# The biases of the second attention, made by GpSimd instead of ScalarE

## The chip, the cores and the metric

The kernel runs on one core of one Trainium2 chip. The metric is the time of one execution on the device, in microseconds. The core has TensorE (PE in the profile), VectorE (DVE), ScalarE (ACT), GpSimd (POOL) and SyncE (SP), which here issues most of the DMAs. Each engine works through its own instructions in order and waits for others by semaphores.

## The reference

The program is one block of a transformer on 256 tokens of width 1024, in float32: a norm, one wide projection, three attentions of 8 heads of 64 (a: stick-breaking, b: "forgetting", c: with a linear position bias), a gate on each, an output projection, and an MLP. Only the second attention matters here:

```
c = lax.cumsum(jax.nn.log_sigmoid(f_logit.astype(jnp.float32)), axis=2)
logits = einsum('bhqd,bhkd->bhqk', qb, kf) * scale + (cq[..., :, None] - c[..., None, :])
p = jax.nn.softmax(jnp.where(causal, logits, NEG_INF), axis=-1)
```

To each logit of query q and key k a bias c[q] - c[k] is added, and keys behind the query are masked.

## The kernel before

Every float32 matrix is split into a high part, rounded to the type float32r, and a low part that holds the rest; three products (high-high, high-low, low-high) are summed in PSUM. So every operand costs two instructions ahead of its matmul: a rounding copy on ScalarE (line 107 for weights, 299 for queries and keys, 361 for attention weights, 379 for attention outputs) and a subtraction on VectorE (lines 110, 300, 362, 380).

Weights come in pieces of 1 MB over SP's queue (line 96, `raw`, two buffers). `pump` splits them ahead of use into up to 7 halves.

The beginning (lines 151 to 331) is in an order written out by hand. Behind it the program text is a list of steps: projections of the pieces of a, b and c one after another, and at given steps the stages of the attention pairs (two heads at a time, four pairs per branch). `forget_bias(pair)` is called at the steps 10, 12, 15 and 17, two steps before the first stage of its pair. The final order on each engine is decided by the framework's planner, from priorities that follow the program text and its own estimates of the costs. It also decides when a buffer is taken.

`forget_terms` makes c: the negated cumulative sums go to DRAM as 8 rows (`c_rows`), and the sums, transposed, to `cq`, a column per head and half of the queries. `forget_bias(pair)` loads for each of two heads its row, broadcast to 128 partitions (`pb`, name `rows`, two buffers, SP's queue, line 491). For each half t of the queries it makes the bias of (t+1) x 128 keys: ScalarE adds the column `cq` to the row (line 497), then GpSimd masks the diagonal block (line 499, `affine_select`). The bias tiles have four buffers, one per head, so the third pair's tiles take those of an earlier pair, once VectorE has read them; four small tiles of the beginning and the third attention's biases (`alibi_bias`, made by GpSimd at line 506) use the same buffers.

`softmax_pair` reads the biases: at line 432 VectorE adds the bias to the logits in PSUM and takes the row minimum of the negated sum, and at line 434 ScalarE takes the exponential.

GpSimd's other work in this part is the zeroing of the padded query and key tiles (lines 288 and 289). Later it has only four short things.

Of the kernel before, what the change touches and what calls it, by code (L numbers as in the profile page):

```python
# [10 lines left out]
AF = mybir.ActivationFunctionType  # L11
ALU = mybir.AluOpType
PSUM = bass.MemoryType.PSUM

P = 128
# [22 lines left out]
def hybrid_attention_block(ctx, tc, x, norm_mix, w_in, b_forget, w_branch, w_out,  # L38
# [4 lines left out]
    nc = tc.nc  # L43
# [406 lines left out]
    forget, bias = {}, {"b": {}, "c": {}}  # L450
# [35 lines left out]
    def forget_bias(pair):  # L486

        rows, cq = forget["c"]
        pb = act.tile([P, 2, S], F32, name="rows", tag="rows", bufs=2)
        for s in range(2):  # L490
            nc.sync.dma_start(pb[:, s], rows[2 * pair + s].partition_broadcast(P))
        for s in range(2):
            h = 2 * pair + s
            b = act.tile([P, 384], F32, name="bias", tag="bias", bufs=4)
            for t in range(NT):
                n = (t + 1) * P
                nc.scalar.activation(b[:, t * P:t * P + n], pb[:, s, 0:n], AF.Identity, bias=cq[:, t, h:h + 1])
                d = slice(2 * t * P, (2 * t + 1) * P)
                nc.gpsimd.affine_select(b[:, d], b[:, d], pattern=[[-1, P]], compare_op=ALU.is_ge, fill=NEG,
                                        base=0, channel_multiplier=1)  # L500
            bias["b"][h] = b
# [47 lines left out]
    for pair, t in enumerate((0, 2, 5, 7)):  # L549
        stages(stick_pair(pair, oT["a"]), (t, t + 3, t + 6))  # L550
        at(WINDOW + t - 2, lambda pair=pair: forget_bias(pair))
        at(2 * WINDOW + t - 2, lambda pair=pair: alibi_bias(pair))
# [194 lines left out]
```

## Time and profile before

| | before |
|---|---|
| median of 3 runs | 464.63 us (464.3 to 466.47) |
| profiled execution | 465.35 us, span of the trace 463.6 us |
| mean granted TensorE clock | 0.998 |
| TensorE busy | 451.0 us (97%) |
| VectorE busy | 324.7 us (70%) |
| ScalarE busy | 274.3 us (59%) |
| GpSimd busy | 38.6 us (8%) |

The span is the time from the first to the last instruction in the trace; the execution's own time has a little around it. TensorE is close to busy all the time: outside the first and the last microseconds it has few waits. The other engines' shares are means over the whole span and are higher in the part with the attentions, up to about 160 us.

### The profile page before, as it was taken

What the parts mean: (1) busy time and instruction counts of PE and PEld (TensorE: products, weight loads), DVE (VectorE), ACT (ScalarE), POOL (GpSimd) and SP (SyncE); (2) the same over time, 40 slices, a digit from 0 to 9 for tenths busy, and PEclk for the clock granted to TensorE, in tenths of its full rate; (3) what the DMA queues carried; (4) which work ended last, traced back from release to release, by engine and by line L of the source; (5) the groups of instructions that cost most, each with busy time, mean ns of one, the idle gap of its engine ahead of it and who ended that gap; (6) DMA issues with size and microseconds to landing.
All of it is one profiled execution on the core that took longest, in us unless ns stands there. A gap on an engine that the chain in (4) does not pass through costs nothing. (4 is left out here: it accounts for less than half of the span.)

```text
span 463.6 us, 6859 instructions
## 1 busy us (share of the span) xinstructions
PE 451.0 (97%) x2575; PEld 392.0 (85%) x2575; DVE 324.7 (70%) x543; ACT 274.3 (59%) x474; POOL 38.6 (8%) x75
## 2 busy tenths in 40 slices
PE   7999999999999999999999998999999999999993
PEld 3989998999899888888888887888888888888882
DVE  5777868788788878658759769778777754444425
ACT  6568998787567876556567346565555533343202
POOL 6501220123000001000000000000000000000012
PEclk9999999999999999999999999999999999999999
DMA  8757644455354448565754808666665555555202
GB/s 288 251 190 232 202 138 159 129 152 176 95 166 151 134 137 275 187 190 170 234 186 134 248 21 251 205 201 195 197 212 184 181 182 182 182 184 183 87 0 91
DMA packets 58001, 80.71 MB, mean 174 GB/s; under 512 B 2520, under 2 KB 45808, under 8 KB 57968
## 3 DMA queue, kind: packets, MB, share of 16 engines
q1 hardware_dynamic: 57632, 79.87, 54.0%
q8 instruction: 20, 0.33, 0.3%
q10 hardware_dynamic: 336, 0.40, 0.2%
q14 instruction: 13, 0.11, 0.1%
HBM read 79.21 MB, written 1.06 MB: 173 GB/s over the span
## 5 line engine op out<-in xcount | busy, mean ns | idle before, releaser
L110 DVE TENSOR_TENSOR wlo_d<-raw,whi_d 128x1024 fp32r<-128x1024 f32 x32 | 39.2, 1226 | 41.5 <-ACT whi_d L107 41.5
L136 PE MATMUL pu<-h,whi_u 128*128 128x512 f32 x256 | 64.6, 393 | 1.2 <-DVE h L239 1.2
L107 ACT ACTIVATE whi_d<-raw 128x1024 fp32r<-128x1024 f32 x32 | 34.0, 1062 | 50.5 <-PE ptok L136 42.4
L136 PEld LDWEIGHTS pu<-h,whi_u 128*128 128x128 f32 x256 | 45.9, 189 | 9.7 <-DVE h L239 1.5
L107 ACT ACTIVATE whi_u<-raw 128x1024 fp32r<-128x1024 f32 x32 | 33.5, 1061 | 29.1 <-PE pu L136 15.6
L136 PE MATMUL ptok<-whi_d,u_lo 128*128 128x512 f32 x128 | 50.5, 395 | 0.0
L136 PE MATMUL ptok<-whi_d,u_hi 128*128 128x512 f32 x128 | 50.5, 394 | 0.0
L110 DVE TENSOR_TENSOR wlo_u<-raw,whi_u 128x1024 fp32r<-128x1024 f32 x32 | 39.0, 1223 | 15.5 <-ACT whi_u L107 15.5
L136 PE MATMUL pg<-hT,whi_g 128*128 128x512 f32 x192 | 48.3, 393 | 0.0
L136 PEld LDWEIGHTS pg<-hT,whi_g 128*128 128x128 f32 x192 | 34.6, 189 | 6.4
L136 PEld LDWEIGHTS pu<-h,wlo_u 128*128 128x128 f32 x256 | 35.2, 190 | 2.6
L110 DVE TENSOR_TENSOR wlo_g<-raw,whi_g 128x1024 fp32r<-128x1024 f32 x24 | 29.4, 1223 | 10.7 <-ACT whi_g L107 9.8
L136 PE MATMUL ptok<-wlo_d,u_hi 128*128 128x512 f32 x128 | 36.9, 395 | 0.0
L136 PE MATMUL pu<-h,wlo_u 128*128 128x256 f32 x256 | 36.0, 282 | 0.0
L107 ACT ACTIVATE whi_g<-raw 128x1024 fp32r<-128x1024 f32 x24 | 25.4, 1060 | 11.9 <-PE pg L136 4.5
L136 PEld LDWEIGHTS ptok<-wlo_d,u_hi 128*128 128x128 f32 x128 | 24.1, 188 | 5.6
L136 PEld LDWEIGHTS ptok<-whi_d,u_hi 128*128 128x128 f32 x128 | 24.1, 188 | 5.6
L136 PEld LDWEIGHTS ptok<-whi_d,u_lo 128*128 128x128 f32 x128 | 24.1, 188 | 5.6
L136 PEld LDWEIGHTS pg<-hT,wlo_g 128*128 128x128 f32 x192 | 26.2, 190 | 1.9
L136 PE MATMUL pg<-hT,wlo_g 128*128 128x256 f32 x192 | 26.8, 282 | 0.0
L705 POOL TENSOR_TENSOR xg<-x,g_fin 128x512 f32<-128x512 f32 x2 | 2.9, 1472 | 268.2 <-issue 266.8
L110 DVE TENSOR_TENSOR wlo_b<-raw,whi_b 128x1024 fp32r<-128x1024 f32 x12 | 14.7, 1225 | 10.4 <-ACT whi_b L107 10.3
(498 smaller groups left out, 940.7 us busy)
## 6 DMA issues: line engine op xcount, KB each, us to landing
raw<-in_w_in_dram SPq DMA_DIRECT2D x29, 1024.0 KB, 5.1
raw<-in_w_up_dram SPq DMA_DIRECT2D x16, 1024.0 KB, 5.6
raw<-in_w_down_dram SPq DMA_DIRECT2D x16, 1024.0 KB, 4.9
raw<-in_w_branch_dram SPq DMA_DIRECT2D x6, 1024.0 KB, 5.0
raw<-in_w_out_dram SPq DMA_DIRECT2D x4, 1024.0 KB, 4.9
x_sb<-in_x_dram SPq DMA_DIRECT2D x2, 512.0 KB, 3.7
raw<-in_w_in_dram SPq DMA_DIRECT2D x2, 512.0 KB, 6.4
rows<-c_rows SPq DMA_DIRECT2D x8, 128.0 KB, 5.7
```

The costliest lines, as they stand in the source:

```text
L107: nc.scalar.activation(hi, raw, AF.Copy)
L110: (nc.gpsimd if n == 0 and i else nc.vector).tensor_tensor(lo, raw, hi.bitcast(F32), op=ALU.subtract)
L136: nc.tensor.matmul(o, l, r, start=first and i == 0, stop=last and i == len(pairs) - 1, **kw)
L705: nc.gpsimd.tensor_tensor(xg[:, d], x1[:, t, d], g_fin[:, d], op=ALU.mult)
```

## The change

In `forget_bias`, the instruction that adds the column to the row is issued on GpSimd rather than ScalarE. GpSimd's `tensor_scalar` has the two operations "add the column" and "add 0.0". The select that follows on the same tile was on GpSimd before, so both are now on one engine. Shapes, buffers, loads and the places of the calls are as before. There are 16 such instructions (8 heads, 2 halves of the queries).

```
@@ -494,7 +494,7 @@
             b = act.tile([P, 384], F32, name="bias", tag="bias", bufs=4)
             for t in range(NT):
                 n = (t + 1) * P
-                nc.scalar.activation(b[:, t * P:t * P + n], pb[:, s, 0:n], AF.Identity, bias=cq[:, t, h:h + 1])
+                nc.gpsimd.tensor_scalar(b[:, t * P:t * P + n], pb[:, s, 0:n], cq[:, t, h:h + 1], 0.0, op0=ALU.add, op1=ALU.add)
                 d = slice(2 * t * P, (2 * t + 1) * P)
                 nc.gpsimd.affine_select(b[:, d], b[:, d], pattern=[[-1, P]], compare_op=ALU.is_ge, fill=NEG,
                                         base=0, channel_multiplier=1)
```

## Rows read from the trace of the kernel before

**Rows 1.** The page: busy time, share of the span, instructions of an engine.

```profile
PE 451.0 (97%) x2575; PEld 392.0 (85%) x2575; DVE 324.7 (70%) x543; ACT 274.3 (59%) x474; POOL 38.6 (8%) x75
```

**Rows 2.** Busy time by stretches (start:end, length, engines, clock, DMA share, GB/s).

```profile
40.00:101.00 61.00, 60.13 (x426) 56.24 (x425) 47.82 (x84) 53.78 (x100) 12.41 (x28) 1.00 0.52 164
```

**Rows 3.** TensorE in order of time: start, us, instruction, [idle before, releaser].

```profile
48.03 2.15 PE L136 MATMUL pqk<-hT,whi_ka 128*128 128x256 f32 x16 [0.42 <-DVE pad_lo L300]
...
67.62 0.47 PE L129 MATMUL po<-s_hi,v_hi 128*128 128x512 f32 x1 [0.45 <-DVE o__211 L380]
```

**Rows 4.** The moved instructions: one row by tile, two by shape.

```profile
L497 ACT ACTIVATE bias<-rows,cq x16: 389/453/516, 43.7 to 99.8; 128x128 f32<-128x128 f32 x8, 128x256 f32<-128x256 f32 x8
...
L497 ACT ACTIVATE bias<-rows,cq 128x256 f32<-128x256 f32 x8 | 4.1, 506 | 0.0
...
L497 ACT ACTIVATE bias<-rows,cq 128x128 f32<-128x128 f32 x8 | 3.2, 399 | 0.0
```

**Rows 5.** GpSimd's operations: by tile (ns min/median/max), and grouped by shape.

```profile
L499 POOL TENSOR_SCALAR_AFFINE_SELECT bias<-bias x16: 288/294/1032, 44.2 to 100.4; 128x128 f32<-128x128 f32 x16
...
L506 POOL TENSOR_SCALAR bias<-rel 128x384 f32<-128x384 f32 x8 | 4.0, 516 | 29.0 <-DVE nm L432 28.8
...
L181 POOL TENSOR_SCALAR_AFFINE_SELECT neg_past<-zeros 128x256 fp32r<-128x256 f32 x1 | 0.4, 408 | 0.0
...
458.29 0.94 POOL L225 TENSOR_TENSOR rstd<-total,minus_half 128x1 f32<-128x1 f32 x1 [1.55 <-DVE total L220]
```

**Rows 6.** GpSimd in order of time (start, us, instruction, idle before).

```profile
44.20 1.28 POOL L499 TENSOR_SCALAR_AFFINE_SELECT bias<-bias 128x128 f32<-128x128 f32 x2 [25.85 <-ACT bias L497]
...
57.36 1.03 POOL L499 TENSOR_SCALAR_AFFINE_SELECT bias<-bias 128x128 f32<-128x128 f32 x2 [0.88 <-ACT bias L497]
...
93.45 0.52 POOL L289 MEMSET pad_lo<- 64x512 f32 x1
...
99.95 0.70 POOL L499 TENSOR_SCALAR_AFFINE_SELECT bias<-bias 128x128 f32<-128x128 f32 x2 [1.75 <-ACT bias L497]
...
113.34 1.11 POOL L506 TENSOR_SCALAR bias<-rel 128x384 f32<-128x384 f32 x2 [0.90 <-DVE nm L432]
...
180.53 1.69 POOL L698 TENSOR_SCALAR g_fin<-g_fin 128x1024 f32<-128x1024 f32 x1 [40.52 <-DMA g_fin<-in_norm_final_dram]
```

**Rows 7.** ScalarE and VectorE in order of time.

```profile
56.89 0.81 ACT L497 ACTIVATE bias<-rows,cq 128x128 f32<-128x128 f32 x2
...
63.96 0.85 ACT L361 ACTIVATE s_hi<-sp 128x768 fp32r<-128x768 f32 x1 [0.89 <-DVE sp L400]
...
110.11 0.38 ACT L299 ACTIVATE pad_hi<-pqk 64x256 fp32r<-64x256 f32 x1
...
41.85 1.23 DVE L110 TENSOR_TENSOR wlo_kb<-raw,whi_kb 128x1024 fp32r<-128x1024 f32 x1 [1.83 <-ACT whi_kb L107]
...
47.45 0.88 DVE L300 SCALAR_TENSOR_TENSOR pad_lo<-pqk,pad_hi 64x256 fp32r<-64x256 f32 x2
...
56.77 1.23 DVE L110 TENSOR_TENSOR wlo_vb<-raw,whi_vb 128x1024 fp32r<-128x1024 f32 x1 [0.35 <-ACT whi_vb L107]
...
61.83 1.23 DVE L110 TENSOR_TENSOR wlo_qb<-raw,whi_qb 128x1024 fp32r<-128x1024 f32 x1 [1.57 <-ACT whi_qb L107]
...
67.05 0.43 DVE L380 TENSOR_TENSOR o__211<-po,o__211 64x256 fp32r<-64x256 f32 x1
```

**Rows 8.** First and last reader of the biases (VectorE); SP's waits for biases.

```profile
85.26 0.28 DVE L432 CUSTOM_DVE_ANT_0 n__1061<-s__1054,bias 128x128 f32<-128x128 f32 x1
...
111.77 0.27 DVE L432 CUSTOM_DVE_ANT_0 n__1467<-s__1460,bias 128x128 f32<-128x128 f32 x1
...
SPq L491 <- ACT bias L497: 4.0, 2, 3.5
```

**Rows 9.** VectorE operations lengthened beside GpSimd (ns min/median/max).

```profile
L110 DVE TENSOR_TENSOR wlo_kc<-raw,whi_kc x4: 1223/1225/1362, 83.5 to 119.3; 128x1024 fp32r<-128x1024 f32 x4
...
L588 DVE TENSOR_TENSOR acc<-acc,sg x4: 683/688/873, 179.1 to 187.3; 128x512 f32<-128x512 f32 x4
```

More of the change, by code (lines that the diff above doesn't have):

```diff
@@ L496, in forget_bias @@
                 n = (t + 1) * P
-                nc.scalar.activation(b[:, t * P:t * P + n], pb[:, s, 0:n], AF.Identity, bias=cq[:, t, h:h + 1])
+                nc.gpsimd.tensor_scalar(b[:, t * P:t * P + n], pb[:, s, 0:n], cq[:, t, h:h + 1], 0.0, op0=ALU.add, op1=ALU.add)
                 d = slice(2 * t * P, (2 * t + 1) * P)
```

## The prediction

> **What bounds the kernel now.** I read the shares of the page first. TensorE is busy 451.0 of 463.6 us, VectorE 324.7, ScalarE 274.3, GpSimd 38.6 [rows 1]. So the question for any change to ScalarE is only whether TensorE waits for it somewhere. The view by stretches comes next: the sixteen ScalarE biases that the change moves run from 43.7 to 99.8 us [rows 4], and from 40 to 101 us TensorE is busy 60.13 of 61.00 us, at a granted clock of 1.00, the full level of 2.4 GHz [rows 2]. ScalarE is the most loaded helper there (53.78 us), VectorE has 47.82, GpSimd 12.41. TensorE in order of time shows two waits in that stretch: 0.42 us at 48.03 for VectorE's `pad_lo` (line 300), and 0.45 us at 67.62 for VectorE's `o_` (line 380) [rows 3]. Their sum, 0.87 us, equals 61.00 - 60.13. That is all that any helper can give back here without a change of TensorE's own work. The chain that ended last covers only the last ten microseconds, and the change does not touch it.
>
> **Part by part: what leaves ScalarE.** The stretch has 8 activations of 128 columns at 399 ns and 8 of 256 at 506 ns [rows 4]: 3.2 + 4.1 = 7.3 us of busy time. Neighbours overlap: the pair at 56.89 takes 0.81 us [rows 7], so 8 such pairs free 6.5 us. The four pairs of the first four heads (3.2 us) lie between 43.7 and 57.7.
>
> What becomes of that time is read at TensorE's two waits. The wait at 67.62 ends a chain. TensorE has finished `pqk` and wants the `po` bank; VectorE frees it at 67.05 + 0.43. In front of that stand, without a gap, a split and line 362, which takes what ScalarE made at 63.96; ScalarE had waited 0.89 us for VectorE's `sp`, and this stands behind a split at 61.83, ahead of which VectorE sat idle 1.57 us for ScalarE's `whi_qb` [rows 7]. ScalarE reached that after the four pairs. I take the chain to move forward by more than 0.45 us, and this wait to go. What is late next is TensorE's own queue: it is full behind. The wait at 48.03 is another matter. VectorE runs without a gap from 41.85 to 48.33, through splits and the like, up to line 300 at 47.45 [rows 7]. Little more than one bias pair (0.81 us) leaves ScalarE before that, and VectorE does not start earlier for it. I leave this 0.42 us where it is. Bounds for this part: 0 (both waits stay) and -0.87 us (both go); value taken -0.45.
>
> **What GpSimd gets.** Sixteen `tensor_scalar` with a per-partition scalar, eight of 128 and eight of 256 columns. GpSimd has this operation with constants: 384 columns in 516 ns; its select of 128x256 took 408 ns, of 128x128 288 to 294 where nothing held it [rows 5]. No row shows the form with a column as scalar. Lower bound: the 516 ns in proportion, 0.17 and 0.34 us. Upper bound: the two-input `tensor_tensor` with `pow`, 0.94 us [rows 5]. I take 0.29 and 0.41 as the rows of the same shapes: 8 x 0.29 + 8 x 0.41 = 5.6 us (4.1 to 15.0), over a stretch in which GpSimd is idle 61.00 - 12.41 = 48.6 us.
>
> None of it is on the path. Of the four pairs, the first is read by VectorE from 85.26 on and the last from 111.77 [rows 8]; the first select is at 44.20, and the last pair's ends at 99.95 + 0.70 = 100.65 [rows 6]. The tightest lead, of the last pair, is 11.1 us. With two adds and two selects per head, even the upper bound (4 x 0.94 + 4 x 1.03 = 7.9 us a pair, with every select held) fits into the 11 us. This lead hides the 5.6 us; if it were gone, one pair's 4 adds and 4 selects (1.4 + 1.2 = 2.6 us) would stand ahead of a softmax.
>
> **New waits and queues.** An add now waits on GpSimd for the row's DMA, for `cq`, and for a free bias buffer; the select no longer waits for another engine. For the third pair the buffer comes free when VectorE has read the first pair's bias (four reads from 85.26 on [rows 8]), and the add waits for that in GpSimd's queue, where zeroings of a padded tile (the last of four at 93.45 [rows 6]) may be behind it. The first user of that tile on ScalarE is at 110.11 [rows 7], 16 us later, so a late zeroing is hidden. On SP, the loads of the rows of pairs 3 and 4 waited 4.0 us for ScalarE's bias of pairs 1 and 2 [rows 8]; they now wait for GpSimd's adds. Weight loads are behind them. Since GpSimd is idle there, I expect these waits to end earlier; the next weight load also waits for its buffer, and thus for VectorE's split at 56.77, to 58.00 [rows 7]. A gain or a loss of up to 4 us on one weight load is hidden, as TensorE nowhere in the stretch waits for a weight [rows 3].
>
> **The port of SBUF.** GpSimd's selects take 288 ns where they are free but up to 1032, and the two at 57.36 take 1.03 us beside VectorE's split at 56.77, which reads two SBUF tensors [rows 5 to 7]. So the new adds will be held in the same way, up to 1 us each, at GpSimd's cost. The other direction is the dangerous one: one split of `kc` took 1362 ns instead of 1225, at 114.16 with GpSimd's biases of 113.34 still running, and one product at line 588 873 ns instead of 688, at 181.88 with GpSimd's `g_fin` of 180.53 running [rows 6, 9]. That is 0.14 to 0.19 us each. With 16 adds the bounds are 0 and 16 x 0.19 = 3.0 us on VectorE, which is idle 61.00 - 47.82 = 13.2 us there and is relieved where it waits for ScalarE. I take 0 for TensorE.
>
> The Trainium skill, page "SBUF — State Buffer", section "Who interferes with whom", says that a VectorE instruction with two SBUF inputs and a GpSimd instruction that reads SBUF exclude each other, and that the second to start is held for all of the first. By that rule a VectorE operation would lose up to the whole of an add, not 0.19 us. The trace agrees on who meets whom, and shows the smaller loss.
>
> **The sum.** The profiled execution took 465.35 us (span 463.6 and 1.75 around it): 465.35 - 0.45 + 0 = 464.9. It lies 0.72 above the median of 464.63, so against the median the forecast is 464.2 us.
>
> **Rivals.** (1) Hidden anyway: the chain to 67.62 is held by VectorE, whose splits stand between its links, and the wait stays. For: VectorE has no gap just ahead of 67.05. Against: the 1.57 us that it waited for ScalarE ahead of 61.83. Time 464.6.
> (2) The port turns it slower: the adds hold VectorE's splits, from 41.85 to 48.33 above all, where VectorE has no gap and TensorE already waits at its end, so that each delay reaches TensorE. Price: 16 x 0.19 = 3.0 us, 467.6; if each add held VectorE for its whole length, 5.6 us, 470.2. It decides once VectorE loses more than its idle time around such a place; a single pair there costs 4 x 0.19 = 0.8 us. For: [rows 9]. Against: the sixteen selects and eight alibi biases of before do the same, and of the four splits of `kc` beside them one was lengthened. The page's rule is this rival at its higher price.
> (3) The planner writes another order on all engines, as it sees ScalarE free earlier. An order that misses links costs waits of the size shown: six of 0.45 us are 2.7, 467.3; against it, weights lie ready well before use. An order that meets them better gains at most the 0.87 us here, 463.8.
> (4) Clearly faster (below 462.3) needs 2.3 us, and TensorE idles 0.87 in the stretch; only waits that the profile does not show could give it.
>
> **How the numbers follow.** Half a per cent, about what a measurement here can tell from no change, is 2.3 us: 462.3 to 466.95. Forecast 0.60 (own range 463.7 to 465.2), hidden anyway 0.20, port 0.08, other order 0.09 (0.05 of it beyond 466.95), clearly faster 0.03. So faster 0.03, within 0.84, slower 0.13. The range reaches down to both waits gone with the fastest of the runs shown (464.3 - 0.87 = 463.4, and a little), and up to 467.0, where the slower cases begin and above the slowest run shown, 466.47.
>
> **What would show it.** Right: ScalarE's busy time 7 us lower, GpSimd's about 6 higher (adds at 0.3 to 0.4 us, longer beside splits); biases ready before 92 and 101; no wait of TensorE for line 380 near 67; the rest of its waits as before. Wrong: VectorE's splits above 1.3 us in number, TensorE waiting for `s_lo`, `pad_lo` or a weight between 40 and 105, or adds of more than 1 us that make line 432 wait for a bias.

## The result, and the profile after

The changed kernel takes 470.85 us in the median (470.56 to 472.4, 4 runs), the kernel before 464.63. The ratio is 1.0137, with a 95% interval of 1.0114 to 1.0161: 6.2 us slower. The forecast was 464.2 us, in a range from about 463.4 to 467.0.

The page's first part, to be read against [rows 1]: TensorE has 3.6 us more busy time in a span 7.1 us longer, ScalarE 5.2 less, GpSimd 23.5 more. The row of the moved instruction, and its two shapes, answer to [rows 4].

```profile
PE 454.6 (97%) x2575; PEld 394.2 (84%) x2575; DVE 325.5 (69%) x543; ACT 269.1 (57%) x458; POOL 62.1 (13%) x91
...
L497 POOL TENSOR_SCALAR bias<-rows,cq x16: 711/1140/2512, 40.8 to 105.9; 128x128 f32<-128x128 f32 x8, 128x256 f32<-128x256 f32 x8
...
L497 POOL TENSOR_SCALAR bias<-rows,cq 128x256 f32<-128x256 f32 x8 | 13.7, 1712 | 0.0
...
L497 POOL TENSOR_SCALAR bias<-rows,cq 128x128 f32<-128x128 f32 x8 | 7.5, 938 | 48.8 <-issue 26.6 <-DMA rows<-c_rows 22.1
```

The adds take 21.2 us, where 5.6 were forecast. Next the stretches of the changed kernel; the first answers to [rows 2].

```profile
40.00:101.00 61.00, 56.42 (x371) 51.99 (x370) 42.40 (x71) 43.28 (x72) 27.30 (x35) 0.94 0.46 149
60.00:70.00 10.00, 7.87 (x62) 7.44 (x60) 3.34 (x5) 3.83 (x6) 1.97 (x4) 1.00 0.72 233
70.00:80.00 10.00, 7.89 (x26) 6.62 (x27) 8.37 (x14) 8.79 (x15) 0.00 (x0) 0.66 0.34 107
71.40:77.90 6.50, 5.79 (x17) 4.95 (x18) 5.13 (x9) 6.35 (x11) 0.00 (x0) 0.50 0.52 161
```

From 60 to 70 us VectorE and ScalarE are busy for little more than a third of the time, and TensorE misses 2.1 us there and 2.1 in the next ten. From 71.4 to 77.9 its granted clock is 0.50, the lower level of 1.2 GHz. TensorE in order of time shows the place; the rows answer to [rows 3].

```profile
66.75 1.12 PE L136 MATMUL pqk<-hT,wlo_kb 128*128 128x256 f32 x8
72.11 0.76 PE L129 MATMUL po<-s_hi,v_hi 128*128 128x512 f32 x1 [4.24 <-DVE o__211 L380]
...
75.88 1.91 PE L136 MATMUL pv<-whi_vb,hT 128*128 128x512 f32 x4
...
78.23 1.09 PE L136 MATMUL pv<-whi_vb,hT 128*128 128x512 f32 x4
...
90.91 2.08 PE L136 MATMUL pqk<-hT,whi_qb 128*128 128x256 f32 x16
```

It is the same instruction as at 67.62 before, waiting for the same bank of PSUM, but 4.24 us instead of 0.45. The bank holds outputs of the first attention, not of the second, whose biases were moved. The clock falls while TensorE waits: it is already at 0.50 from 71.4. From `po` at 72.11 to the second `pv` group at 78.23 is 6.12 us; in the kernel before, the same work ran from 67.62 to this row, 3.45 us:

```profile
71.07 1.07 PE L136 MATMUL pv<-whi_vb,hT 128*128 128x512 f32 x4
```

So the wait costs 3.8 us more than before and the half clock 2.7: 6.5 of the 7.1 us between the two profiled executions. Most of the rest lies ahead of 37 us, where the execution of the changed kernel is 0.8 us longer.

The chain behind the wait, from its end to its start: VectorE and ScalarE of the changed kernel, in order of time, answering to [rows 7]:

```profile
60.59 0.96 DVE L400 SCALAR_TENSOR_TENSOR sp<-z,e 128x768 f32<-128x768 f32 x1 [1.50 <-ACT e L398]
67.62 1.23 DVE L110 TENSOR_TENSOR wlo_qb<-raw,whi_qb 128x1024 fp32r<-128x1024 f32 x1 [6.08 <-ACT whi_qb L107]
68.76 0.95 DVE L362 TENSOR_TENSOR s_lo<-sp,s_hi 128x768 fp32r<-128x768 f32 x1
...
70.30 1.21 DVE L110 TENSOR_TENSOR wlo_qb<-raw,whi_qb 128x1024 fp32r<-128x1024 f32 x1
71.54 0.43 DVE L380 TENSOR_TENSOR o__211<-po,o__211 64x256 fp32r<-64x256 f32 x1
...
66.53 1.06 ACT L107 ACTIVATE whi_qb<-raw 128x1024 fp32r<-128x1024 f32 x1 [5.97 <-DMA raw<-in_w_in_dram]
67.50 0.37 ACT L299 ACTIVATE qk_hi<-pqk 128x256 fp32r<-128x256 f32 x1
67.76 0.83 ACT L361 ACTIVATE s_hi<-sp 128x768 fp32r<-128x768 f32 x1
68.49 0.36 ACT L379 ACTIVATE o__211<-po 64x256 fp32r<-64x256 f32 x1
...
70.41 0.38 ACT L379 ACTIVATE o__211<-po 64x256 fp32r<-64x256 f32 x1 [0.61 <-DVE o__211 L380]
```

ScalarE stands 5.97 us before the rounding of `whi_qb`, for a weight that has not landed. TensorE needs that weight only at 90.91, 24 us after the rounding starts. But behind the rounding, in ScalarE's order, stand the two copies of `o_` (68.49 and 70.41), and behind the subtractions on VectorE (67.62 and 70.30) the low halves of them; the second, at 71.54, frees the bank.

Why the weight is late stands in SP's queue: first the changed kernel, with SP's waits from 40 to 75 us, then the kernel before.

```profile
44.65 0.38 SPq L96 DMA_DIRECT2D raw<-in_w_in_dram  x1
49.05 10.49 SPq L491 DMA_DIRECT2D rows<-c_rows  x4
59.59 50.54 SPq L96 DMA_DIRECT2D raw<-in_w_in_dram  x8
...
SPq L491 <- POOL bias L497: 8.8, 1, 8.8
```

```profile
45.11 7.47 SPq L96 DMA_DIRECT2D raw<-in_w_in_dram  x2
53.17 4.87 SPq L491 DMA_DIRECT2D rows<-c_rows  x3
58.13 0.39 SPq L96 DMA_DIRECT2D raw<-in_w_in_dram  x1
```

Before, two weight pieces went out ahead of the rows of pairs 3 and 4. In the changed kernel the planner has written all four row loads ahead of the second piece (`qb`). The last two need the buffer of pair 2's rows, and GpSimd's last add for that pair reads it until 58.7:

```profile
46.11 2.91 POOL L497 TENSOR_SCALAR bias<-rows,cq 128x128 f32<-128x128 f32 x2 [0.38 <-DMA rows<-c_rows]
...
56.53 2.18 POOL L497 TENSOR_SCALAR bias<-rows,cq 128x256 f32<-128x256 f32 x1
```

So `qb` goes out at 59.59, and not by 52.58 (45.11 + 7.47) as before: 7 us later. That is the reading; the runs test each link.

### The profile page after: what moved, and what is told of

It reads as the page before. It is cut to its first block, busy times and chain, and to the rows that moved or that the text cites. A ratio compares the mean times of both kernels' runs of the same rounds, so it can differ in the third digit from the quotient of the medians.

```text
span 470.7 us, 6856 instructions
## 1 busy us (share of the span) xinstructions
PE 454.6 (97%) x2575; PEld 394.2 (84%) x2575; DVE 325.5 (69%) x543; ACT 269.1 (57%) x458; POOL 62.1 (13%) x91
## 5 line engine op out<-in xcount | busy, mean ns | idle before, releaser
L110 DVE TENSOR_TENSOR wlo_u<-raw,whi_u 128x1024 fp32r<-128x1024 f32 x32 | 38.9, 1223 | 15.8 <-ACT whi_u L107 15.7
L497 POOL TENSOR_SCALAR bias<-rows,cq 128x128 f32<-128x128 f32 (+1 forms) x16 | 21.1, 1325 | 48.8 <-issue 26.6
```

What stands on the lines that cost most here:

```text
L110: (nc.gpsimd if n == 0 and i else nc.vector).tensor_tensor(lo, raw, hi.bitcast(F32), op=ALU.subtract)
L497: nc.gpsimd.tensor_scalar(b[:, t * P:t * P + n], pb[:, s, 0:n], cq[:, t, h:h + 1], 0.0, op0=ALU.add, op1=ALU.add)
```

## The experiments

Diffs are against the changed kernel unless they say otherwise; medians and ratios are against the kernel before on the same chip. Hunks are shown in part; `follow(a, b)` puts a behind b in the order of one engine.

**Four row buffers.** The adds stay as slow. Not shown is the room for it: three small tiles take other tiles' buffers.

```
-        pb = act.tile([P, 2, S], F32, name="rows", tag="rows", bufs=2)
+        pb = act.tile([P, 2, S], F32, name="rows", tag="rows", bufs=4)
```

> The changed kernel with four buffers for the rows instead of two (three small rows of forget_terms share other tiles' buffers, to make room); the adds stay on GpSimd and stay slow, and the order on TensorE, VectorE, ScalarE and GpSimd is the same. Theory A (queue): the loss comes from SP, where four row loads wait 8.8 us for GpSimd to free their buffers, ahead of the weight piece qb; with free buffers nothing waits there, TensorE's wait of 4.24 us and the half clock behind it go, and the time is 464 to 465.5 us. Rival B (port of SBUF: slow adds hold VectorE) and rival C (the new order on ScalarE and VectorE): no difference, 470 to 471.5 us.

464.52 us against 464.58, ratio 0.9992 (0.9976 to 1.0009). All of the loss is gone. The stretch, GpSimd's adds, and SP's queue:

```profile
40.00:101.00 61.00, 61.00 (x438) 57.49 (x437) 49.19 (x84) 49.40 (x86) 33.95 (x43) 1.00 0.48 160
...
L497 POOL TENSOR_SCALAR bias<-rows,cq 128x256 f32<-128x256 f32 x8 | 12.6, 1578 | 0.0
...
43.81 0.98 SPq L491 DMA_DIRECT2D rows<-c_rows  x2
50.24 24.55 SPq L96 DMA_DIRECT2D raw<-in_w_in_dram  x4
```

GpSimd is busy 33.95 us, and its 256-column adds still take 1.58 us, yet TensorE does not wait once. No row load waits for a bias, and `qb` goes out at 50.24. So neither the slow adds (rival B, the port) nor the new order on the other engines (rival C, the same order in this trace) costs anything by itself; the loss needs the held queue.

**SP's order of before.** Two buffers, slow adds; only the order of the loads is put back.

```
-                nc.sync.dma_start(state["raw"], src)
+                state["load", which, br, j] = nc.sync.dma_start(state["raw"], src)
...
-            nc.sync.dma_start(pb[:, s], rows[2 * pair + s].partition_broadcast(P))
+            load = nc.sync.dma_start(pb[:, s], rows[2 * pair + s].partition_broadcast(P))
+            if pair > 1:
+                follow(load, state["load", "k" if (pair, s) == (3, 1) else "q", "b", 1])
```

> The changed kernel with its two row buffers and slow adds, but with the order on SP as in the kernel before: the weight piece qb goes ahead of the rows of pairs 3 and 4, and kb ahead of the last of them. All other engines have the order of the changed kernel. Theory A: the weight qb lands before it is wanted, as before, and the time is 464 to 465.5 us. Rivals B and C: 470 to 471.5 us.

464.74 us, ratio 1.0006 (0.9991 to 1.0021). SP still waits 4.5 us for GpSimd, but with `qb` already out:

```profile
44.46 7.37 SPq L96 DMA_DIRECT2D raw<-in_w_in_dram  x2
51.92 5.92 SPq L490 DMA_DIRECT2D rows<-c_rows  x3
57.93 0.39 SPq L96 DMA_DIRECT2D raw<-in_w_in_dram  x1
...
SPq L490 <- POOL bias L498: 4.5, 1, 4.5
```

In the two traces the other engines have the same order, so the order of one queue is the whole difference between 470.85 and 464.74 us.

**Constants for the column.** SP's bad order stays.

```
-                nc.gpsimd.tensor_scalar(b[:, t * P:t * P + n], pb[:, s, 0:n], cq[:, t, h:h + 1], 0.0, op0=ALU.add, op1=ALU.add)
+                nc.gpsimd.tensor_scalar(b[:, t * P:t * P + n], pb[:, s, 0:n], 1.0, 0.0, op0=ALU.mult, op1=ALU.add)
```

> The changed kernel with constants (times 1, plus 0) in place of the column in GpSimd's instruction: the column, one number for each row of the softmax, is left out of the bias. Order of the work on every engine as in the changed kernel, four row loads ahead of the weight included. The price of the column form by itself: theory A says 0.3 and 0.4 us in place of 0.94 and 1.71, so the rows are free by about 50 us, SP waits under 3 us, and the time is 464 to 465.5 us. Rival B: GpSimd still reads SBUF as often, though shorter: 466 to 469 us. Rival C: 470 to 471.5 us.

464.61 us, ratio 1.0005 (0.9986 to 1.0023). The adds and SP's row loads:

```profile
L497 POOL TENSOR_SCALAR bias<-rows 128x256 f32<-128x256 f32 x8 | 4.6, 581 | 0.0
...
L497 POOL TENSOR_SCALAR bias<-rows 128x128 f32<-128x128 f32 x8 | 3.0, 380 | 42.2 <-DMA rows<-c_rows 22.5 <-issue 19.4 <-POOL pad_lo L289 0.3
...
44.96 7.51 SPq L491 DMA_DIRECT2D rows<-c_rows  x4
52.52 22.74 SPq L96 DMA_DIRECT2D raw<-in_w_in_dram  x4
```

With adds of 0.38 and 0.58 us the buffers come free at 51.65, and `qb` goes out at 52.52, as before. SP's wait for GpSimd, forecast under 3 us, was 6.6, but it ended in time. Hence both are needed for the loss: the bad order and the slow form. At the price that the prediction assumed, the change is harmless.

**More work for TensorE.** The projection ahead of the wait is done twice, with the same result.

```
-            terms(p_, [(w[a][:, k], hT[:, k, b]) for a, b in ((0, 0), (0, 1), (1, 0)) for k in range(KD)], True, True)
+            for _ in range(2 if (which, br, quad, j) == ("k", "b", 0, 1) else 1):
+                terms(p_, [(w[a][:, k], hT[:, k, b]) for a, b in ((0, 0), (0, 1), (1, 0)) for k in range(KD)], True, True)
```

> The changed kernel in which TensorE does the projection kb (half 1), the work directly ahead of its wait of 4.24 us, twice: 24 matmuls, 3.1 us, with the same result. Theory A1 (4.24 us of the loss are the wait, and the other some 2.9 us are the half clock of 5.9 us that follows the idle time): the doubled work lies inside the wait, TensorE idles only some 1.1 us, the clock stays full, and the kernel gets faster with more work: 467.5 to 468.7 us. Rival A2 (the half clock has nothing to do with the idle time): 470.5 to 471.5 us; rival A3 (the doubled work delays what follows): 473 to 474.

467.74 us, ratio 1.0072 (1.0048 to 1.0095): 3.1 us faster than the changed kernel, with 24 matmuls more. The second pass and what follows it:

```profile
67.99 2.08 PE L136 MATMUL pqk<-hT,whi_kb 128*128 128x256 f32 x16
69.91 1.12 PE L136 MATMUL pqk<-hT,wlo_kb 128*128 128x256 f32 x8
70.99 0.47 PE L129 MATMUL po<-s_hi,v_hi 128*128 128x512 f32 x1
...
70.00:80.00 10.00, 10.00 (x54) 8.52 (x53) 7.88 (x13) 9.31 (x15) 0.00 (x0) 1.00 0.32 107
```

ScalarE still stands 5.29 us for the weight there, but TensorE works on, and the clock stays at 1.00. So the half clock belongs to the idle time. The excess over the kernel before, 3.16 us, is the second pass, 2.9 us (65.13 to 67.99 for the first), and little else. The rest of the wait, 1.4 us by the changed kernel's 4.24 and forecast as some 1.1, did not appear: in this execution ScalarE began the rounding 1.1 us earlier (65.40), and TensorE came to this work 0.3 us later.

**The rounding behind the copies.** Slow adds and SP's bad order stay; ScalarE rounds the late weight only behind the copies that free the bank, and the planner moves the subtraction and a few neighbours with it.

```
-                nc.scalar.activation(hi, raw, AF.Copy)
+                state["round", which, br, j, i] = nc.scalar.activation(hi, raw, AF.Copy)
...
-            nc.scalar.activation(o[r, pair, 0], src, AF.Copy)
+            copy = nc.scalar.activation(o[r, pair, 0], src, AF.Copy)
+            if pair == 0 and s == 1 and o is oT["a"]:
+                follow(state["round", "q", "b", 1, 0], copy)
```

> The changed kernel, with slow adds, two row buffers and the row loads ahead of the weight on SP, but ScalarE rounds the late weight qb (half 0) only behind the copies of the first pair's output (line 379); the planner moves the subtraction on VectorE with it. Theory A (the weight is first used by TensorE some 15 us later, and the loss comes from what stands behind its rounding and subtraction on ScalarE and VectorE): SP's wait of 8 to 9 us stays, TensorE's wait is below 1 us and the time 464 to 466 us. Rival A' (the weight itself comes too late): 470 to 471.5 us.

465.69 us, ratio 1.0015 (0.9992 to 1.0039). ScalarE in order of time, TensorE's one wait from 40 to 105 us, and SP's wait:

```profile
61.69 0.38 ACT L378 ACTIVATE o__211<-po 64x256 fp32r<-64x256 f32 x1 [1.09 <-DVE o__211 L381]
63.65 2.01 ACT L107 ACTIVATE whi_qb<-raw 128x1024 fp32r<-128x1024 f32 x2 [1.58 <-DMA raw<-in_w_in_dram]
...
PE pv L136 <- DVE pad_lo L300: 0.6, 1, 0.6
...
SPq L491 <- POOL bias L497: 8.1, 1, 8.1
```

SP waits 8.1 us, nearly as long as in the changed kernel, and the loss is gone but for a part that this run can't tell from nothing. The rounding starts 2.9 us earlier than in the changed kernel, and TensorE reaches the work ahead of `po` 1.4 us earlier: counted from TensorE's place, the weight comes 1.5 us less late. With the old order some 2.8 us of the wait of 4.24 would have been left, by estimate; 0.6 is, and at another place.

**The kernel before, with SP's bad order.** The diff is against the kernel before; the biases are on ScalarE.

```
-                nc.sync.dma_start(state["raw"], src)
+                state["load", which, br, j] = nc.sync.dma_start(state["raw"], src)
...
-            nc.sync.dma_start(pb[:, s], rows[2 * pair + s].partition_broadcast(P))
+            load = nc.sync.dma_start(pb[:, s], rows[2 * pair + s].partition_broadcast(P))
+        if pair == 3:
+            follow(state["load", "q", "b", 1], load)
```

> The kernel before, biases on ScalarE, with the order of the changed kernel on SP: all row loads of pairs 3 and 4 ahead of the weight qb. The planner sees that weight late and moves its rounding behind line 379 by itself. Theory A: SP waits some 8 us for ScalarE's biases (the last ends at 57.7), the weight comes about as late as in the changed kernel, and the time is still 464 to 466 us, as nothing that TensorE needs stands behind the rounding. Rival A' (a late weight costs by itself): 469 to 471 us.

464.44 us, ratio 0.9999 (0.9977 to 1.002).

```profile
64.07 0.38 ACT L379 ACTIVATE o__211<-po 64x256 fp32r<-64x256 f32 x1
65.78 2.01 ACT L107 ACTIVATE whi_qb<-raw 128x1024 fp32r<-128x1024 f32 x2 [1.33 <-DMA raw<-in_w_in_dram]
...
SPq L490 <- ACT bias L498: 11.2, 2, 7.6
```

SP waits 11.2 us for the biases, in two pieces, and the rounding starts at 65.78, within 0.8 us of the changed kernel's 66.53. TensorE is 1.5 us later in this execution, so the weight comes 2.2 us less late than there, and the old order would still have left a wait of some 2 us, by estimate; TensorE has none between 40 and 105 us. So a weight this late costs nothing by itself, and in the changed kernel too TensorE wants it only at 90.91. What costs is what stands behind its rounding: here the planner has put the rounding behind both copies (64.07 is the second), while in the changed kernel the first rounding is ahead of both.

**Two other forms of the add**, both with four row buffers, one run each.

```
+ nc.gpsimd.tensor_scalar(b[...], pb[...], cq[:, t, h:h + 1], None, op0=ALU.add)
```

> As the run with four row buffers, but the add is one operation with the column, without the second (plus 0.0): the price of the form. If the column is slow: 0.71 us for 128 and 1.14 us for 256 columns where nothing holds it, as with two operations; if the second operation is: 0.30 and 0.43. Time 464 to 466 us either way.

```
+ nc.gpsimd.tensor_tensor(b[...], pb[...], cq[:, t, h:h + 1].to_broadcast([P, n]), op=ALU.add)
```

> As the run with four row buffers, but the add is GpSimd's two-input form, with the column repeated along the row. From the two-input product of 512 columns, 1.47 us: 0.37 us for 128 and 0.74 for 256 columns, if the repeated column costs nothing more; as much as the column form, 0.71 and 1.14, if the column is what is slow. Time 464 to 466 us.

The two kernels' adds by tile (ns min/median/max; the first row is the one operation):

```profile
L497 POOL TENSOR_SCALAR bias<-rows,cq x16: 601/928/2005, 39.5 to 97.7; 128x128 f32<-128x128 f32 x8, 128x256 f32<-128x256 f32 x8
```

```profile
L497 POOL TENSOR_TENSOR bias<-rows,cq x16: 392/608/1322, 39.8 to 96.3; 128x128 f32<-128x128 f32 x8, 128x256 f32<-128x256 f32 x8
```

Times 464.56 and 465.5 us. The least of each row is for 128 columns; for 256 the least are 920 and 607 ns. Both answers to the first question were partly wrong: leaving out the second operation takes 128 columns from 711 to 601 ns, so it is the column that costs most. The two-input form with a repeated column, 392 ns, is nearly twice as fast as the form with a column (711). The forecast of 0.37 us for it held, 0.74 for 256 columns was too high (0.61).

**The version that this points to**: four row buffers and constants.

> The version that the runs so far point to: four row buffers, GpSimd's add with constants (the column, which is the same number along a row of the softmax, is left out of the bias). If the forecast's gain is real (the two waits of TensorE, 0.87 us, gone, with nothing given back): 463.7 to 464.2 us against some 464.55 of the kernel before, ratio 0.998 to 0.999. If TensorE's two waits are made up elsewhere: 464.4 to 464.8 us, ratio 1.000. In either case no step beyond half a per cent.

464.62 us against 464.16, ratio 1.0008 (0.9991 to 1.0025): no better than the kernel before. No version beat it by more than can be measured.

## Why the prediction was wrong

**What was read right.** TensorE's waits decide, and ScalarE's relief was worth little. ScalarE's busy time fell by 5.2 us in total, 7.3 forecast for the moved instructions; the biases stayed far ahead of their readers (the last pair's by 9.0 us, 11.1 before).

**The price of the add failed first.** "I take 0.29 and 0.41 as the rows of the same shapes": where nothing held them they measured 0.71 and 1.14, and in the mean 0.94 and 1.71, beyond the upper bound of 0.94 for the wide ones. Rows with constants, and a select, were taken for a form that no row showed, and the bound came from a one-column operation, which says nothing on the price per column.

**The step that made the loss is "New waits and queues".** It said of the row loads "I expect these waits to end earlier" and "A gain or a loss of up to 4 us on one weight load is hidden, as TensorE nowhere in the stretch waits for a weight". The first assumed that SP's order would stay, and that GpSimd would be quick; the waits grew from 4.0 us [rows 8] to 8.8 in one piece, and the weight behind them came 7 us later, not up to 4. The second looked for TensorE's own waits for weights. But a late weight acts through ScalarE's and VectorE's orders, where its rounding and subtraction stand in front of the copies that free `po`. The prediction had this very chain in hand (67.05 behind a split behind `whi_qb`) and used it only for a gain. Putting back SP's order, freeing the buffers, quick adds, or a rounding placed behind the copies each took the loss away.

**The clock was left out.** The rivals priced a wait at its own length. In the wait of 4.24 us the clock fell, and the work from its end at 72.11 to 77.9 ran at half clock, 2.7 us more.

**The rivals.** The port (2) was not the cause: with adds as slow and as many, four buffers gave 464.52. Another order by the planner (3) was the right kind of cause, with a chance of 0.09 and the wrong price, six waits of 0.45 us, where it was one long wait on one queue.

**The forecast gain of 0.45 us** can't be seen. The wait at 67.62 is gone in the profiles of the first three experiments, as is the one at 48.03, yet their ratios are 0.9992, 1.0006 and 1.0005. The traces tell more. From the first `neg_past` matmul (line 389, 35.99 us before the change) to the last matmul, TensorE takes 420.1 us before, and 418.5 to 418.7 in these three; but it takes 418.7 also in the kernel before with SP's bad order, whose biases are on ScalarE. So the two waits cost some 0.7 us each in that execution, more than the 0.87 us in all that the prediction allowed, and can go, but their going is no sign of ScalarE's relief. The beginning ahead of that matmul took 35.9 to 38.9 us. Of the nine kernels that are left without the changed one and the one with more work for TensorE, the three whose beginning took less than 36 us have waits of some 0.4 us or more between 40 and 105 us, and the other six have none. This looks as if TensorE meets these waits when it comes early; with one trace of each kernel, and no run made for it, that is not shown.

## What to carry to other kernels

When an engine that frees a buffer becomes slower, look at the queue that waits for that buffer and at everything behind it, prefetches too, and then at what stands behind the first use of those prefetches on each engine: an early weight that is late is no loss to TensorE, but the instruction that prepares it can hold the ones that TensorE waits for. When a planner writes the order, compare the order of each queue before and after, and do not assume it. Price a new instruction form by a row of that form, or keep the bound wide.

## What the runs showed of the hardware that was not expected

GpSimd's add with a per-partition column: 711 ns for 128 columns and 1138 for 256, so some 3.3 ns a column; with constants 298 and 407 ns, 0.85 a column; with two inputs and the column repeated 392 and 608, 1.7 a column. The Trainium skill, page "GPSIMD Engine Reference", section "Engine selection", says that against VectorE GpSimd is about twice as slow with two inputs and roughly at line rate with one. For two inputs the trace agrees: the one subtraction of a weight half that the kernel before has on GpSimd (`wlo_qa`, line 110) took 2428 ns, and 1225 is usual for this shape on VectorE [rows 9]. For one tensor and a column it does not: one operation of 128 columns took 601 ns on GpSimd where nothing held it, and the same shape of VectorE's product with a column (line 438) 270 at the least; there the measurement decides.

Beside VectorE's operations with two SBUF inputs the column adds took up to 2512 ns, 1.4 us more than alone, while VectorE's splits of `vc` took up to 1370 ns, 1262 in the median of four. As before the change [rows 9], GpSimd loses much and VectorE up to some 0.19 us.
